# One ring of seven for weight and conditioning tiles, and the shifted S5 inputs regrouped through DRAM, in a two-layer trunk on one core

## The chip, the cores and the metric

The kernel runs on one core of one Trainium2 chip. The metric is device time in microseconds (us). Before the change it is 2463.67 us, the median of three runs (2461.16 to 2466.41). One execution was profiled; it took 2467.97 us, of which its span on the chip is 2466.1 us. A tile in this text is one 512 KB load, 128 partitions of 1024 fp32 numbers, unless it is called something else.

## The reference

Two layers act on x (256 tokens of 2048 numbers). Layer 0 mixes tokens with stick-breaking attention, layer 1 with S5, a diagonal complex state-space layer; each is followed by an MLP with squared ReLU. Every sub-layer is normalised, shifted, scaled and gated by vectors that come from the conditioning vector c.

```python
for i in range(DEPTH):
    mod = cond @ ada_w[i] + ada_b[i]
    sh1, sc1, g1, sh2, sc2, g2 = jnp.split(mod, 6, axis=-1)
    h = modulate(rmsnorm(x, ln1_g[i]), sh1, sc1)
    y = stick_breaking_mixer(...) if i == 0 else s5_mixer(...)
    x = x + g1[:, None, :] * y
    h = modulate(rmsnorm(x, ln2_g[i]), sh2, sc2)
    x = x + g2[:, None, :] * sq_relu_mlp(h, mlp_w1[i], mlp_w2[i])
```

S5 projects h to u (`w_in`), groups 16 channels to a state of 64 complex numbers, runs the recurrence over the tokens, adds `d_skip * u`, applies GELU and then a gated linear unit (`w_glu`), whose result is y. All weights are fp32, so one execution reads some 600 MB.

## The kernel before

Two streams of tiles come in from HBM on one queue, that of SyncE (SP).

**Weights.** `weights` (L126) loads a tile into `w`, ScalarE (ACT) copies it to `wh`, a rounded fp32r number, and VectorE (DVE) takes the difference `wl` (L133). TensorE (PE) then multiplies three times: `wl` by the high part, `wh` by the low part and `wh` by the high part of the activations. One call of `cols_tile` (L152) is one tile and 24 such matmuls, and ends a tick of the program (`tick`, L101). `w` has three buffers (`self.nw = 3`), `wh` and `wl` have three each (`self.nh`).

**Conditioning.** `ada_load` (L262) loads tiles of `ada_w` into `adaw`, a ring of its own with four buffers (eight in the first stage). DVE multiplies each by one number per partition and adds it to a running sum (L356, L370): one instruction and one tile are a unit. `pump` (L240) hands out units at `self.rate` per tick: 1.0 from the first MLP on, 0.42 after the function `between`, 0.35 in the S5 mixer, and in the GLU `pace(44, ...)`, which spreads what is still missing over 44 ticks. `drain` does at once what has to be ready.

The order within PE and POOL is as written. On SP, ACT and DVE a scheduler places each instruction by its readiness and by when a buffer of its ring comes free, and the queue then runs in that order, each instruction waiting for those ahead of it.

The stages are attention (to about 496 us), the first MLP (256 tiles, here MLP0), S5 (32 tiles of `w_in`), GLU (64 tiles of `w_glu`) and the second MLP (256 tiles, MLP1).

**S5.** Eight groups of four ticks each give `acc`, in which two blocks of 128 channels stand; there are 16 blocks `bi`. For each block a plan of delays, counted in ticks (`at`), issues:

- `s5_windows`: DVE scales `acc` into `u` (L1029), ACT adds the shift (L1030). Four zero columns stand ahead of the 256 tokens.
- `s5_shuffle`, one tick later: 16 matmuls against columns of the identity move four channel groups and four shifts of u into PSUM, and ACT copies them to `imc` (L1040). [...]
- `s5_operands`, one tick later as well, and `s5_states`, two ticks later: eight matmuls of `imc` (L1053) and then seven DVE instructions (L1055 to L1063, with the scan L1060). The table T that they read is loaded on SP (L1000) into a ring of two.
- `s5_outputs`, six ticks later, and `s5_taps`, four ticks later.

```python
for q in range(4):
    for j in range(4):
        nc.tensor.matmul(pi[32 * j:32 * j + 32, 65 * q:65 * q + 65], self.ident[:, 32 * q:32 * q + 32],
                         uw[:, 4 - j:4 - j + 257:4], start=True, stop=True)
```

Of the kernel before, what the change touches and what calls it, by code (L numbers as in the profile page):

```python
# [8 lines left out]
F32 = mybir.dt.float32  # L9
# [3 lines left out]
AF = mybir.ActivationFunctionType  # L13
OP = mybir.AluOpType
AX = mybir.AxisListType

P = 128
D = 2048
NB = D // P
S = 256  # L20
# [36 lines left out]
class Trunk:  # L57
# [203 lines left out]

    def ada_load(self, layer, vec, g, t, wide=False):  # L262
        start = g == 0 and vec < 2 and layer == 0
        wt = (self.ap0 if start else self.wp).tile([P, 2, 512], F32, name="adaw", bufs=8 if start else 4)
        c0 = vec * D + g * 512
        w = self.i["ada_w"][layer]
        if wide:
            self.nc.sync.dma_start(wt, w[t * P:t * P + P, c0:c0 + 1024].rearrange("p (a b) -> p a b", a=2))
        else:
            self.nc.sync.dma_start(wt, w[2 * t * P:2 * t * P + 2 * P, c0:c0 + 512].rearrange("(a p) b -> p a b", p=P))  # L270
        return wt
# [630 lines left out]
    def s5_open(self, sp):  # L902
        g_ = self.nc.gpsimd
        self.sE = sp.tile([P, 2, 4, 4, 2, 16], F32, name="E")
        self.sCA = [sp.tile([P, 2, 4, 4, 2, 16], F32, name="CA%d" % k) for k in range(3)]
        self.sKL = [sp.tile([P, 3, 4, 2, 16], F32, name="KL%d" % k) for k in range(3)]
        self.simc = [sp.tile([P, 4, 65], F32, name="imc%d" % k) for k in range(3)]
        self.sU = [sp.tile([P, 4 + S + 1], F32, name="u%d" % k) for k in range(3)]
        self.sM = [sp.tile([P, 2, 4, 64], F32, name="M%d" % k) for k in range(2)]
        self.sP = [sp.tile([P, 224], F32, name="taps%d" % k) for k in range(2)]  # L910
        for t in [self.sE] + self.sP + self.sM + self.sCA + [u[:, 0:4] for u in self.sU]:
            g_.memset(t, 0.0)
        self.sS = {}

# [108 lines left out]
            nc.tensor.transpose(pk[:, tau * P - P:tau * P], self.sP[bi % 2][:, o:o + P], self.ident)  # L1023
        nc.scalar.activation(self.sKL[bi % 3].rearrange("p t q a e -> p (t q a e)"), pk[:, :3 * P], AF.Copy)

    def s5_windows(self, bi, acc):
        nc = self.nc
        uw = self.sU[bi % 3]
        nc.vector.tensor_tensor(uw[:, 4:], acc[:, :S + 1], self.rms, op=OP.mult)  # L1029
        nc.scalar.activation(uw[:, 4:4 + S], uw[:, 4:4 + S], AF.Identity, bias=uw[:, 4 + S:])  # L1030

    def s5_shuffle(self, bi):
        nc = self.nc
        uw, imc = self.sU[bi % 3], self.simc[bi % 3]
        pi = self.mp()
        for q in range(4):
            for j in range(4):
                nc.tensor.matmul(pi[32 * j:32 * j + 32, 65 * q:65 * q + 65], self.ident[:, 32 * q:32 * q + 32],  # L1038
                                 uw[:, 4 - j:4 - j + 257:4], start=True, stop=True)
        nc.scalar.activation(imc.rearrange("p q k -> p (q k)"), pi[:, :4 * 65], AF.Copy)  # L1040

    def s5_states(self, sp, bi):
        nc, s5 = self.nc, self.s5
# [20 lines left out]

    def s5_outputs(self, sp, bi):
        nc = self.nc
        u, St = self.sU[bi % 3][:, 4:4 + S], self.sS.pop((bi, "R")).rearrange("p c (q k) -> p c q k", q=4)
        CA, KL, imc = self.sCA[bi % 3], self.sKL[bi % 3], self.simc[bi % 3]
        py = self.mp()
        for tau in range(4):  # L1070
            for c in range(2 if tau == 0 else 3):
                for q in range(4):
                    o = py[32 * q:32 * q + 32, 64 * tau:64 * tau + 64]
                    if c < 2:
                        lhs, rhs = CA[:, c, q, tau], St[:, c, q]
                    else:
                        lhs, rhs = KL[:, tau - 1, q], imc[:, q, 1:65]
                    nc.tensor.matmul(o, lhs.rearrange("p a e -> p (a e)"), rhs, start=(c == 0), stop=(c == (2 if tau else 1)))  # L1078
        nc.vector.scalar_tensor_tensor(u.rearrange("p (k i) -> p i k", i=4), u.rearrange("p (k i) -> p i k", i=4),
                                       self.dcol[:, bi:bi + 1], py[:, 0:S].rearrange("p (i k) -> p i k", i=4),  # L1080
                                       op0=OP.mult, op1=OP.add)
        nc.scalar.activation(self.z[:, bi], u, AF.Gelu_apprx_tanh)
        if not self.split_z:
            self.sdone.add(bi)
        else:
            self.split(self.hH[:, bi, :S], self.hL[:, bi, :S], self.z[:, bi])

    def s5_mixer(self, mid):
        nc, tc = self.nc, self.tc
        w_in, w_glu = self.i["s5_w_in"][0], self.i["s5_w_glu"][0]  # L1090
        st = ExitStack()
        sp = st.enter_context(tc.tile_pool(name="s5", bufs=1, reuse_waits="tile"))
# [7 lines left out]
        for gi in range(8):  # L1100
            acc = self.accs()
            if gi < 7:
                self.at(2, self.s5_load, sp, gi + 1)
            for b in range(2):
                bi = 2 * gi + b
                t = 4 + 2 * b
                self.at(t + 6, self.s5_outputs, sp, bi)
                self.at(t - 0, self.s5_expand, sp, bi)
                self.at(t, self.s5_windows, bi, acc[:, b])
                self.at(t + 1, self.s5_operands, sp, bi)  # L1110
                self.at(t + 1, self.s5_shuffle, bi)
                self.at(t + 2, self.s5_states, sp, bi)
                self.at(t + 4, self.s5_taps, bi)
            for t in range(4):
                self.cols_tile(acc, w_in, gi * 256, t, hH, hL)
# [16 lines left out]
        a, b = self.gemm_two(w_glu, D, 0, *z, before)  # L1132
        with tc.tile_pool(name="glu", bufs=2, reuse_waits="tile") as gp:
            for g in range(8):
# [4 lines left out]
                if g:  # L1139
                    b = self.gemm_cols(w_glu, g * 256, *z)  # L1140
# [41 lines left out]

    def run(self):
        nc = self.nc
        self.nw, self.nh = 3, 3
        self.rate, self.credit, self.pending = 0.0, 0.0, {}
        self.recorder, self.early = None, True
        self.left, self.acts, self.unit, self.sums, self.turn = {}, [], 0, None, 0
# [56 lines left out]

        self.mlp(0, nxt=ready, between=between)
        self.dump("x2")
        self.rate = 0.35
        self.s5_mixer(mid)
        self.dump("x3")  # L1250
        self.logexp()
# [32 lines left out]
```

## Time and profile before

| what | value |
|---|---|
| median of three runs | 2463.67 us |
| profiled execution, and its span | 2467.97 us, 2466.1 us |
| PE busy | 2365.1 us (96%) |
| DVE busy | 1795.4 us (73%) |
| ACT busy | 1212.7 us (49%) |
| POOL busy | 316.6 us (13%) |
| read from HBM | 607 MB, with the rest 253 GB/s over the span |

PE is shown busy for 96% of the span. These ends are modelled and matmuls overlap, so the number of matmul records in a stretch says more than the busy time; some records can be missing. DMA is the busy share of the 16 DMA engines. `PEclk` is the granted TensorE clock as a part of 2.4 GHz. A row such as "PE acc L160 <- DVE wl L133" says that PE stood idle and what released it. Idle time of an engine off the path costs nothing, and a busy share is an average over stages that differ.

### The profile page before, as it was taken

The numbers are of one execution on the slowest core, as the hardware profiler recorded it, in microseconds if no ns is written. First come the engines' busy times: TensorE is split into PE (matmuls) and PEld (weight loads), VectorE is DVE, ScalarE is ACT, GpSimd is POOL, SyncE is SP. The second block draws the span as 40 slices with busy tenths as digits, with TensorE's granted clock in tenths as the row PEclk, the third lists the DMA queues.
The fourth block names the chain that finished last, engine by engine and source line by source line (L and its number), as shares of the span: only waits on it lengthen the run. The fifth ranks groups of instructions, "written<-read, shape, count | busy, mean of one in ns | idle before, by whom it ended". The sixth has DMA issues, their size and how long they took to land.

```text
span 2466.1 us, 45235 instructions
## 1 busy us (share of the span) xinstructions
PE 2365.1 (96%) x18355; PEld 2160.4 (88%) x18355; DVE 1795.4 (73%) x2223; ACT 1212.7 (49%) x1814; POOL 316.6 (13%) x340
## 2 busy tenths in 40 slices
PE   7999999999998999889999999989999999999999
PEld 4777789899988899889998998989998998998987
DVE  5789999999778767875786668888744554555554
ACT  4534875346334335435546776434554543543543
POOL 0000110001056545445300000000000000000000
PEclk9999999999999999999999999999999999999999
DMA  9888899999999967997798544999856555556565
GB/s 341 302 299 306 288 308 320 322 303 294 310 310 315 300 207 230 309 299 219 259 316 276 174 154 159 314 329 314 281 175 192 184 186 190 175 179 193 180 195 164
DMA packets 416773, 627.09 MB, mean 254 GB/s; under 512 B 19858, under 2 KB 282420, under 8 KB 414260
## 3 DMA queue, kind: packets, MB, share of 16 engines
q1 hardware_dynamic: 411968, 606.16, 74.8%
q0 software_dynamic: 3968, 17.83, 2.2%
q8 instruction: 144, 2.36, 0.4%
q14 instruction: 65, 0.53, 0.1%
q10 hardware_dynamic: 628, 0.21, 0.0%
HBM read 607.34 MB, written 16.78 MB: 253 GB/s over the span
## 4 chain that ended last, share of the span: by engine, by line
PE 44%; DMA 6%; DVE 5%; issue 3%; ACT 0%; SPq 0%; DVEq 0%; ACTq 0%
PE acc L160 9%; PE acc L162 8%; PE acc L161 8%; DMA adaw<-in_ada_w 5%; PE acc L146 5%; PE acc L148 5%; PE acc L147 5%; DVE wl L133 2%; PE mp L1053 1%; DVE adsums L356 1%; PE mp L1078 1%; PE mp L1038 1%; PE mp L1015 1%; DVE xT L435 1%; DMA w<-in_s_w_glu 0%
## 5 line engine op out<-in xcount | busy, mean ns | idle before, releaser
L131 ACT ACTIVATE wh<-w 128x1024 fp32r<-128x1024 f32 x736 | 777.5, 1058 | 1030.9 <-PE acc L162 364.6
L133 DVE TENSOR_TENSOR wl<-w,wh 128x1024 fp32r<-128x1024 f32 x736 | 922.6, 1255 | 436.9 <-ACT wh L131 434.3
L160 PE MATMUL acc<-hH,wl 128*128 128x258 f32 (+1 forms) x2816 | 808.4, 287 | 28.4 <-DVE wl L133 26.1
L162 PE MATMUL acc<-hH,wh 128*128 128x258 f32 (+1 forms) x2816 | 799.2, 284 | 0.0
L161 PE MATMUL acc<-hL,wh 128*128 128x258 f32 (+1 forms) x2816 | 797.8, 283 | 0.2 <-DVE hL L123 0.2
L160 PEld LDWEIGHTS acc<-hH,wl 128*128 128x128 f32 x2816 | 535.8, 190 | 44.3 <-DVE wl L133 33.6
L161 PEld LDWEIGHTS acc<-hL,wh 128*128 128x128 f32 x2816 | 536.3, 190 | 0.6 <-DVE hL L123 0.4
L162 PEld LDWEIGHTS acc<-hH,wh 128*128 128x128 f32 x2816 | 534.8, 190 | 0.0
L160 PE MATMUL acc<-aH,wl 128*128 128x256 f32 x1024 | 294.3, 287 | 26.4 <-DVE wl L133 25.5
L161 PE MATMUL acc<-aL,wh 128*128 128x256 f32 x1024 | 289.5, 283 | 0.0
L162 PE MATMUL acc<-aH,wh 128*128 128x256 f32 x1024 | 289.4, 283 | 0.0
L356 DVE SCALAR_TENSOR_TENSOR adsums<-adaw,cond,adsums 128x1024 f32<-128x1024 f32 x150 | 199.1, 1328 | 53.6 <-DMA adaw<-in_ada_w 53.0
L160 PEld LDWEIGHTS acc<-aH,wl 128*128 128x128 f32 x1024 | 194.3, 190 | 34.1 <-DVE wl L133 33.7
L146 PE MATMUL acc<-wh,aL 128*128 128x512 f32 x512 | 202.2, 395 | 0.0
L148 PE MATMUL acc<-wh,aH 128*128 128x512 f32 x512 | 202.1, 395 | 0.0
L147 PE MATMUL acc<-wl,aH 128*128 128x512 f32 x512 | 202.0, 395 | 0.0
L161 PEld LDWEIGHTS acc<-aL,wh 128*128 128x128 f32 x1024 | 194.4, 190 | 0.0
L162 PEld LDWEIGHTS acc<-aH,wh 128*128 128x128 f32 x1024 | 194.2, 190 | 0.0
L370 DVE SCALAR_TENSOR_TENSOR adacc<-adaw,cond,adacc 128x512 f32<-128x512 f32 x240 | 179.2, 750 | 3.1 <-DMA adaw<-in_ada_w 1.3
L146 PE MATMUL acc<-wh,hL 128*128 128x512 f32 x384 | 157.5, 410 | 5.8 <-ACT wh L131 3.1
L147 PE MATMUL acc<-wl,hH 128*128 128x512 f32 x384 | 153.8, 401 | 3.3 <-DVE wl L133 3.2
L148 PE MATMUL acc<-wh,hH 128*128 128x512 f32 x384 | 152.9, 398 | 0.0
(311 smaller groups left out, 2751.0 us busy)
## 6 DMA issues: line engine op xcount, KB each, us to landing
w<-in_mlp_w SPq DMA_DIRECT2D x512, 512.0 KB, 4.0
adaw<-in_ada_w SPq DMA_DIRECT2D x384, 512.0 KB, 6.0
w<-in_sb_w_in SPq DMA_DIRECT2D x96, 512.0 KB, 5.2
w<-in_s_w_glu SPq DMA_DIRECT2D x64, 512.0 KB, 5.4
w<-in_sb_w_out SPq DMA_DIRECT2D x32, 512.0 KB, 5.7
w<-in_s_w_in SPq DMA_DIRECT2D x32, 512.0 KB, 4.8
pw<-W POOLq DMA_DIRECT2D x8, 1024.0 KB, 6.5
W<-pw SPq DMA_DIRECT2D x8, 1024.0 KB, 7.7
```

Of the source, the lines that this page charges most:

```text
L131: nc.scalar.activation(h, w, AF.Copy)
L133: nc.vector.tensor_tensor(l, w, h.bitcast(F32), op=OP.subtract)
L146: nc.tensor.matmul(o, aL(kb)[:, s], H[:, kk], start=(kb == k0), stop=False)
L147: nc.tensor.matmul(o, aH(kb)[:, s], L[:, kk], start=False, stop=False)
L148: nc.tensor.matmul(o, aH(kb)[:, s], H[:, kk], start=False, stop=(kb == k1 - 1))
L160: nc.tensor.matmul(o, L[:, kk, s], aH(kb), start=(kb == k0), stop=False)
L161: nc.tensor.matmul(o, H[:, kk, s], aL(kb), start=False, stop=False)
L162: nc.tensor.matmul(o, H[:, kk, s], aH(kb), start=False, stop=(kb == k1 - 1))
L356: nc.vector.scalar_tensor_tensor(acc, wt, c, acc, op0=OP.mult, op1=OP.add)
L370: nc.vector.scalar_tensor_tensor(acc, wt[:, kk], c, acc, op0=OP.mult, op1=OP.add)
L435: nc.vector.scalar_tensor_tensor(x, y, self.mod[layer][:, vec * 16 + kb:vec * 16 + kb + 1], x, op0=OP.mult, op1=OP.add)
L1015: nc.tensor.transpose(pe[:, q * P:q * P + P], E[:, c, q].rearrange("p j a e -> p (j a e)"), self.ident)
```

## The change

Three things change.

1. `adaw` outside the first stage is no ring of its own any more: conditioning tiles and weight tiles take turns in one ring `w` of seven buffers (`self.nw = 7`). It holds as many bytes as the three and four before.
2. The shuffle on PE goes. `s5_inputs` scales into a scratch tile `uw` (one buffer), ACT writes u with the four token phases apart (`i k`) and stores it in DRAM (`um`) from its own queue. `s5_regroup`, one tick later, reads it back on SP in four pieces, one for each shift. Column 0 of `imc` stays zero. `s5_states` comes three ticks after the inputs, where it came after two.
3. The rate of conditioning units in the S5 mixer is 0.6, where it was 0.35.

`s5_outputs` now reads u and PSUM in the same order and leaves the reordering to the GELU on ACT.

```diff
 def ada_load(self, layer, vec, g, t, wide=False):
     start = g == 0 and vec < 2 and layer == 0
-    wt = (self.ap0 if start else self.wp).tile([P, 2, 512], F32, name="adaw", bufs=8 if start else 4)
+    wt = self.ap0.tile([P, 2, 512], F32, name="adaw", bufs=8) if start else self.wp.tile([P, 2, 512], F32, name="w", bufs=self.nw)
...
-        self.sU = [sp.tile([P, 4 + S + 1], F32, name="u%d" % k) for k in range(3)]
+        self.sU = [sp.tile([P, S], F32, name="u%d" % k) for k in range(3)]
+        self.um = [self.dram.tile([P, S], F32, name="um%d" % bi) for bi in range(16)]
...
-        for t in [self.sE] + self.sP + self.sM + self.sCA + [u[:, 0:4] for u in self.sU]:
+        for t in [self.sE] + self.sP + self.sM + self.sCA + self.simc:
             g_.memset(t, 0.0)
...
-    def s5_windows(self, bi, acc):
-        nc = self.nc
-        uw = self.sU[bi % 3]
-        nc.vector.tensor_tensor(uw[:, 4:], acc[:, :S + 1], self.rms, op=OP.mult)
-        nc.scalar.activation(uw[:, 4:4 + S], uw[:, 4:4 + S], AF.Identity, bias=uw[:, 4 + S:])
-
-    def s5_shuffle(self, bi):
-        nc = self.nc
-        uw, imc = self.sU[bi % 3], self.simc[bi % 3]
-        pi = self.mp()
-        for q in range(4):
-            for j in range(4):
-                nc.tensor.matmul(pi[32 * j:32 * j + 32, 65 * q:65 * q + 65], self.ident[:, 32 * q:32 * q + 32],
-                                 uw[:, 4 - j:4 - j + 257:4], start=True, stop=True)
-        nc.scalar.activation(imc.rearrange("p q k -> p (q k)"), pi[:, :4 * 65], AF.Copy)
+    def s5_inputs(self, sp, bi, acc):
+        nc = self.nc
+        uw, u = sp.tile([P, S + 1], F32, name="uw", bufs=1), self.sU[bi % 3]
+        nc.vector.tensor_tensor(uw, acc[:, :S + 1], self.rms, op=OP.mult)
+        nc.scalar.activation(u.rearrange("p (i k) -> p i k", i=4), uw[:, :S].rearrange("p (k i) -> p i k", i=4), AF.Identity, bias=uw[:, S:])
+        nc.scalar.dma_start(self.um[bi], u)
+
+    def s5_regroup(self, bi):
+        nc, imc = self.nc, self.simc[bi % 3]
+        src = self.um[bi].rearrange("(q p) (i k) -> i p q k", q=4, i=4)
+        for j in range(4):
+            o = 1 if j else 0
+            nc.sync.dma_start(imc[32 * j:32 * j + 32, :, o:o + 64], src[(4 - j) % 4])
...
-        nc.vector.scalar_tensor_tensor(u.rearrange("p (k i) -> p i k", i=4), u.rearrange("p (k i) -> p i k", i=4),
-                                       self.dcol[:, bi:bi + 1], py[:, 0:S].rearrange("p (i k) -> p i k", i=4),
-                                       op0=OP.mult, op1=OP.add)
-        nc.scalar.activation(self.z[:, bi], u, AF.Gelu_apprx_tanh)
+        nc.vector.scalar_tensor_tensor(u, u, self.dcol[:, bi:bi + 1], py[:, 0:S], op0=OP.mult, op1=OP.add)
+        nc.scalar.activation(self.z[:, bi].rearrange("p (k i) -> p i k", i=4), u.rearrange("p (i k) -> p i k", i=4), AF.Gelu_apprx_tanh)
...
-                self.at(t, self.s5_windows, bi, acc[:, b])
+                self.at(t, self.s5_inputs, sp, bi, acc[:, b])
                 self.at(t + 1, self.s5_operands, sp, bi)
-                self.at(t + 1, self.s5_shuffle, bi)
-                self.at(t + 2, self.s5_states, sp, bi)
+                self.at(t + 1, self.s5_regroup, bi)
+                self.at(t + 3, self.s5_states, sp, bi)
...
-        self.nw, self.nh = 3, 3
+        self.nw, self.nh = 7, 3
...
-        self.rate = 0.35
+        self.rate = 0.6
         self.s5_mixer(mid)
```

The order of the loads on SP shows what the one ring does. The first place is MLP0, from its 64th weight tile on; `in_ada_w` is a conditioning tile, `in_mlp_w` a weight tile. Before:

```order
L268 DMA adaw<-in_ada_w 128x1024
L129 DMA w<-in_mlp_w 128x4x256
L268 DMA adaw<-in_ada_w 128x1024
L129 DMA w<-in_mlp_w 128x4x256
L268 DMA adaw<-in_ada_w 128x1024
L129 DMA w<-in_mlp_w 128x4x256 x2
L268 DMA adaw<-in_ada_w 128x1024
L129 DMA w<-in_mlp_w 128x4x256
```

The same place now:

```order
L268 DMA w<-in_ada_w 128x1024
L129 DMA w<-in_mlp_w 128x4x256 x3
L268 DMA w<-in_ada_w 128x1024
L129 DMA w<-in_mlp_w 128x4x256 x2
L268 DMA w<-in_ada_w 128x1024
L129 DMA w<-in_mlp_w 128x4x256 x2
L268 DMA w<-in_ada_w 128x1024
L129 DMA w<-in_mlp_w 128x4x256 x3
```

Before, conditioning tiles had run ahead of the rate of 0.42 and stood nearly one to one with weight tiles, with long runs of weight tiles alone elsewhere. Now they stand at the rate. Counted over the whole listing, MLP0 has 146 conditioning tiles before and 117 now, S5 has 7 and 20, GLU has 59 and 60, MLP1 has 17 and 32.

The second place is the middle of S5 on SP; `in_s_w_in` is a weight tile, T and W are tables of S5. Before, from the 17th weight tile on:

```order
L917 DMA W<-pw_5451 128x2048
L1000 DMA T<-rot_5436 128x768
L129 DMA w<-in_s_w_in 128x4x256 x2
L1000 DMA T<-rot_5437 128x768
L129 DMA w<-in_s_w_in 128x4x256 x2
L917 DMA W<-pw_5452 128x2048
```

Now, where the number behind `um` counts the blocks:

```order
L1039 DMA imc_14058<-um_14067 32x4x64 x4
L1001 DMA T<-rot_5437 128x768
L268 DMA w<-in_ada_w 128x1024
L129 DMA w<-in_s_w_in 128x4x256
L918 DMA W<-pw_5452 128x2048
L1039 DMA imc_14059<-um_14068 32x4x64 x4
L129 DMA w<-in_s_w_in 128x4x256
L1001 DMA T<-rot_5438 128x768
L268 DMA w<-in_ada_w 128x1024
L129 DMA w<-in_s_w_in 128x4x256
```

Four reads of `imc` and one or two conditioning tiles have come into each block. When the reads of a block are issued, three to seven weight tiles beyond its own group of four ticks have been issued ahead of them.

The third place is the end of GLU (`in_s_w_glu`) and the start of MLP1 on SP. Before:

```order
L129 DMA w<-in_s_w_glu 128x4x256
L268 DMA adaw<-in_ada_w 128x1024
L129 DMA w<-in_s_w_glu 128x4x256
L268 DMA adaw<-in_ada_w 128x1024
L129 DMA w<-in_mlp_w 128x4x256 x2
L268 DMA adaw<-in_ada_w 128x1024
L129 DMA w<-in_mlp_w 128x4x256
```

Now:

```order
L268 DMA w<-in_ada_w 128x1024 x2
L129 DMA w<-in_s_w_glu 128x4x256
L268 DMA w<-in_ada_w 128x1024
L129 DMA w<-in_s_w_glu 128x4x256
L268 DMA w<-in_ada_w 128x1024
L129 DMA w<-in_s_w_glu 128x4x256 x21
L129 DMA w<-in_mlp_w 128x4x256 x5
```

The 60 conditioning tiles of GLU now stand among its first 43 weight tiles, and the last 21 stand alone. Before, the first 8 weight tiles stood alone and the 59 were spread over the rest.

## Rows read from the trace of the kernel before

**Rows 1.** Windows: us; busy (x) of PE, PEld, DVE, ACT, POOL; clock, DMA, GB/s.
```profile
20.00:320.00 300.00, 288.40 (x1322) 216.61 (x1321) 254.50 (x438) 166.72 (x325) 11.04 (x17) 0.98 0.89 305
...
620.00:1290.00 670.00, 633.17 (x5166) 621.48 (x5165) 513.61 (x510) 291.24 (x359) 273.09 (x274) 0.99 0.85 279
1290.00:1530.00 240.00, 232.71 (x3602) 215.77 (x3605) 168.92 (x233) 162.54 (x329) 5.13 (x11) 0.99 0.58 186
1530.00:1800.00 270.00, 252.32 (x2123) 246.85 (x2112) 221.48 (x245) 121.79 (x160) 0.00 (x0) 0.98 0.90 306
1800.00:2466.00 666.00, 660.07 (x4058) 590.52 (x4056) 346.59 (x319) 302.73 (x348) 0.00 (x0) 1.00 0.59 183
```

**Rows 2.** Waits of PE in 620:1290: us in total, times, longest.
```profile
PE acc L160 <- DVE wl L133: 35.9, 30, 3.2
```

**Rows 3.** Windows: two stretches of 60 us within MLP0.
```profile
1020.00:1080.00 60.00, 52.31 (x422) 50.28 (x421) 48.73 (x45) 17.62 (x18) 38.35 (x36) 1.00 0.92 306
...
1140.00:1200.00 60.00, 60.00 (x504) 60.00 (x503) 37.72 (x38) 33.06 (x44) 21.71 (x23) 1.00 0.68 210
```

**Rows 4.** Waits in 1020:1080.
```profile
ACT wh L131 <- DMA w<-in_mlp_w: 33.2, 14, 5.4
```

**Rows 5.** Windows of 620:1290 for L356, then for L133: us, DVE busy (x).
```profile
620.00:1290.00 670.00, 144.03 (x103) 0.99 0.85 279
...
620.00:1290.00 670.00, 280.46 (x212) 0.99 0.85 279
```

**Rows 6.** Timeline of PE in S5: start us, us, then the instruction.
```profile
1401.32 1.13 PE L1038 MATMUL mp<-u,ident 128*32 128x65 f32 x32
1402.38 0.39 PE L160 MATMUL acc<-hH,wl 128*128 128x258 f32 x1
...
1413.55 1.13 PE L1038 MATMUL mp<-u,ident 128*32 128x65 f32 x32
```

**Rows 7.** Groups of instructions on DVE: busy us, mean ns of one.
```profile
L133 DVE TENSOR_TENSOR wl<-w,wh 128x1024 fp32r<-128x1024 f32 x736 | 922.6, 1255 | 436.9 <-ACT wh L131 434.3 <-PE acc L162 0.7
...
L356 DVE SCALAR_TENSOR_TENSOR adsums<-adaw,cond,adsums 128x1024 f32<-128x1024 f32 x150 | 199.1, 1328 | 53.6 <-DMA adaw<-in_ada_w 53.0
...
L1060 DVE TENSOR_TENSOR_SCAN R<-M,R 128x512 f32<-128x512 f32 x16 | 19.6, 1224 | 0.7
...
L1055 DVE TENSOR_TENSOR w<-mp,T 128x512 f32<-128x512 f32 x16 | 11.0, 690 | 12.7 <-PE mp L1053 12.7
...
L1079 DVE SCALAR_TENSOR_TENSOR u<-u,colv,mp 128x256 f32<-128x256 f32 x16 | 10.9, 682 | 0.0
```

**Rows 8.** Groups of the split on ACT and of the S5 inputs.
```profile
L131 ACT ACTIVATE wh<-w 128x1024 fp32r<-128x1024 f32 x736 | 777.5, 1058 | 1030.9 <-PE acc L162 364.6 <-DMA w<-in_mlp_w 240.3 <-PE acc L148 236.7
...
L1030 ACT ACTIVATE u<-u 128x256 f32<-128x256 f32 x16 | 8.1, 508 | 15.2 <-DVE u L1029 15.2
...
L1029 DVE TENSOR_TENSOR u<-acc,rms 128x257 f32<-128x257 f32 x16 | 6.7, 420 | 9.9 <-PE acc L162 9.3 <-ACT z L1082 0.5
```

**Rows 9.** DMA issues: count, KB each, median us from issue to landing.
```profile
rot<-turns POOLq DMA_DIRECT2D x16, 384.0 KB, 4.9
T<-rot SPq DMA_DIRECT2D x16, 384.0 KB, 3.6
```

**Rows 10.** Timeline of the SP queue: start us, us that one issue takes.
```profile
1500.56 0.34 SPq L1000 DMA_DIRECT2D T<-rot  x1
```

**Rows 11.** Waits of the SP queue over the whole span.
```profile
SPq L1000 <- DVE w L1062: 60.2, 13, 5.6
```

**Rows 12.** Windows within GLU.
```profile
1540.00:1720.00 180.00, 167.96 (x1364) 163.19 (x1364) 152.52 (x173) 73.47 (x94) 0.00 (x0) 0.99 0.93 318
1590.00:1650.00 60.00, 51.17 (x411) 49.54 (x411) 56.81 (x72) 23.86 (x34) 0.00 (x0) 0.99 1.01 357
```

**Rows 13.** Windows of 1590:1650 for L133, then for L356.
```profile
1590.00:1650.00 60.00, 19.51 (x16) 0.99 1.01 357
...
1590.00:1650.00 60.00, 29.03 (x24) 0.99 1.01 357
```

More of the change, by code (lines that the diff above doesn't have):

```diff
@@ L1066, in s5_outputs @@
         nc = self.nc
-        u, St = self.sU[bi % 3][:, 4:4 + S], self.sS.pop((bi, "R")).rearrange("p c (q k) -> p c q k", q=4)
+        u, St = self.sU[bi % 3], self.sS.pop((bi, "R")).rearrange("p c (q k) -> p c q k", q=4)
         CA, KL, imc = self.sCA[bi % 3], self.sKL[bi % 3], self.simc[bi % 3]
```

## The prediction

> **What bounds the kernel now.** I read the windows by stage first, then PE's waits within a stage, then the loads behind them. The reader should see four regimes in [rows 1]. Attention (20:320) has DVE busy 254.5 of 300 us. MLP0 and GLU (620:1290, 1530:1800) have the DMA engines busy 85% and 90%, with PE below full. S5 (1290:1530) and MLP1 (from 1800 on) have them at 58% and 59%, and MLP1 has PE at 660.07 of 666 us: there is nothing to gain there.
>
> In MLP0 PE's only wait is for `wl`, 35.9 us in 30 pieces [rows 2]. Two stretches of it tell why. From 1140 to 1200, where no conditioning tile is read, PE makes 504 matmul records in 60 us, 0.119 us each, so a tile of 24 costs 2.86 us [rows 3]. From 1020 to 1080 it makes 422, at 306 GB/s and 92% DMA share [rows 3], and ACT waits 33.2 us for weights that have not landed [rows 4]. The loss is 82 records, 9.8 us of 60. So conditioning tiles in bursts starve PE while other stretches have room.
>
> **MLP0: the one ring.** The stage made 5166 records in 670 us [rows 1]; at 0.119 us they need 615 us, so 55 us are lost. It consumed 212 weight and 103 conditioning tiles [rows 5], 0.49 to one on average, but nearly one to one where the order before bunches them. Now they stand at 0.43, evenly (seven to sixteen in the listing). Demand, worked out: 212 + 92 tiles of 0.524 MB in 615 us are 259 GB/s. To this comes other traffic: 279 GB/s times 670 us are 187 MB, less 315 tiles (165 MB) leaves 22 MB, 36 GB/s. Together 295 GB/s, below the 357 GB/s that the DMA engines reach in GLU [rows 12], though not far below the 306 of the starved stretch [rows 3]. DVE then needs 1.26 us per weight tile and 0.43 x 1.33 us for conditioning [rows 7], 1.83 of 2.86 us. What hid nothing before was the depth: with three weight buffers a late tile showed at once; now about five of the seven hold weights.
>
> Of the 55 us I take back 30 of the 35.9 us of waits, 4 of the 6.7 us that a granted clock of 0.99 over 670 us means (parts of it ran at the lower level, 1.2 GHz), and 2 of the 12 us left, which the trace does not explain: 36 us. The bounds are 15 (the DMA engines still late half of the time, since 295 is near 306) and 52 (all but the small rest).
>
> **S5: PE's part.** The shuffle of a block starts at 1401.32 and the next tile at 1402.38, so it holds PE for 1.06 us [rows 6]; 16 of them are 17 us. The eviction to `imc` on ACT goes too, on an engine that is not late. The blocks follow each other every 12.23 us (1401.32 to 1413.55) [rows 6]; without the shuffle, 11.17.
>
> What stands beside it: DVE has per block two `wl` (2.51 us), the scan (1.22), six multiplies and adds like L1055 (0.69 each, 4.14), the scaling (0.42, [rows 8]), the output (at most 0.68) and, new, 20 conditioning tiles over 16 blocks (1.25 x 1.33 = 1.66) [rows 7]. That is 10.63 of 11.17 us, 95%, on a queue that waits in order for PE's states. I expect 0.4 us lost per block, 7 us, so S5 gives 10 us. Bounds: 17 given, or a loss if the round trip is late (below).
>
> **S5: the round trip.** The wait that is new sits on SP: the four reads wait for the store, and weights queue behind them. The trace before has no such store from ACT; the nearest rows are the store of 384 KB from POOL, 4.9 us, and the read of T on SP, 3.6 us [rows 9]. The chain is 0.42 (DVE) + 0.51 (ACT) + one `wh` ahead of the store (1.06) [rows 8] + 4.9 + 3.6 = 10.5 us, and 4 x 0.34 = 1.4 us for issuing four reads [rows 10]: 11.9 us. Against it, PE has three tiles (8.6 us) and at least one full set of S5 work (11.17 - 5.72 = 5.45 us) between inputs and states: 14 us. So it fits by 2 us for the first block of a group; the second has two ticks more. For the weights behind the reads the cover is larger: three to seven tiles beyond the group are issued ahead of them. That SP can stand still is shown: it waits 60.2 us in 13 pieces for T's buffer [rows 11], while PE in S5 is 232.71 of 240 us busy. I take nothing for this wait; its upper bound is rival B.
>
> On this the Trainium skill speaks against the change: "DMA: Bandwidth & Descriptors", section "Anatomy of one DMA", says that a transfer's signal comes only when the last byte is confirmed, which takes longest where HBM is the target. No row here shows a small store to HBM alone. By that section's fit (2.0 us plus bytes over 436 GB/s; an estimate) the store would take 2.3 and the reads 2.1 us, the chain 7.8 us, and rival B would be less likely; its caution about HBM pulls the other way.
>
> **GLU: what comes back.** Conditioning work not done early in MLP0 falls here. From 1540 to 1720 PE made 1364 records where 180 us allow 1513, so 17.7 us are lost now [rows 12]. From 1590 to 1650, 24 conditioning and 16 weight tiles go through DVE [rows 13] in 60 us at 101% DMA share: 1.5 us per tile of either kind, DVE at 56.81 of 60 [rows 12]. That is the price of this mixture on both engines. Now 60 conditioning tiles stand among 43 weight tiles: 103 x 1.5 = 155 us against 43 x 2.86 = 123, 32 lost instead of 17.7, less some 2 us for what the ring holds when the stage begins: 12 us worse. Bounds: 0 (the seven buffers smooth it) and 25 (DVE's order adds to it).
>
> **The rest.** At the end of GLU DVE is free of conditioning, so the sum of squares that PE waits for should come sooner: 2 us. MLP1 gets 15 conditioning tiles more over half its ticks, under a DMA share of 59%: nothing. Attention keeps its 139 tiles and its DVE time: nothing, plus or minus 6.
>
> **Sum.** -36 - 10 + 12 - 2 = -36 us on the profiled 2467.97, so 2432 there. The profiled run lies 4.3 us above the median, which gives 2463.67 - 36 = 2428 us.
>
> **Rivals.**
> - A, the DMA engines bound MLP0 whatever the order. For it: 306 GB/s was all that the starved stretch got, with POOL's tables moving beside. Against it: GLU ran at 357. MLP0 gives 15 instead of 36: 2449 us.
> - B, slower: the round trip sets the pace of S5. Place: the states on PE, which wait for `imc`, with DVE and its `wl` in order behind. For it: the margin is 2 us, and SP already waits up to 5.6 us for T [rows 11]; 11.9 + 5.6 = 17.5 us are 3.5 too late, 16 times, 56 us. That gives -36 + 56 = +20: 2484 us. It decides from 36 / 16 = 2.3 us of lateness per block. Against it: the second block of each group has more room, and T's wait precedes only some reads.
> - C, DVE becomes the bound in S5 and GLU, at 95% in both: S5 gives 0, GLU costs 25. -36 + 0 + 25 - 2 = -13: 2451 us.
> - D, everything fits: -52 - 17 + 5 - 4 = -68: 2396 us.
> That the ring does nothing is no rival, since the order on SP has changed as shown.
>
> **How the numbers follow.** Forecast 0.58, A 0.14, C 0.12, B 0.08, D 0.08. The forecast's own range is 2410 to 2446. The 8-in-10 range runs from 2398 to 2458: it takes in A and C and half of D and leaves out B. No change means within 0.2%, 4.9 us, about what a measurement can tell. Faster: the forecast, D, and nine tenths of A and C less a little, 0.86. Within 0.2%: the upper edges of A and C and a quarter of B, 0.06. Slower: most of B and the rest, 0.08.
>
> **What would show it.** Right: in MLP0 PE's wait for `wl` falls from 35.9 us to under 10 with 0.43 conditioning tiles per weight tile; blocks in S5 follow each other at 11.2 to 11.8 us; in GLU PE loses some 30 us in its first two thirds and none in its last; MLP1 is unchanged. Wrong: PE waiting for `imc`, or SP waiting for the store while ACT waits for weights (B); 306 GB/s and the old waits in MLP0 (A); a block of 12 us in S5 with DVE never idle (C). If MLP0 gives less than 20 us or S5 takes longer than before, the forecast fails at that step.

## The result: 2.7% slower

| | before | after |
|---|---|---|
| median, us (runs) | 2463.99 (4) | 2530.32 (4), 2526.79 to 2537.05 |
| ratio, 95% interval | | 1.0273 [1.0248, 1.0298] |
| span of the profiled run, us | 2466.1 | 2525.0 |

The forecast was 2428 us, with a range of 2398 to 2458. The stages below are differences between first starts in the timelines: the evictions to `half` (first group of MLP0), the first `rl` of its second group, the first S5 input (L1029, after: L1030), the first and the last `sg` of GLU.

| us | attention | MLP0, first group | MLP0, rest | S5 | GLU | rest |
|---|---|---|---|---|---|---|
| before | 503.1 | 214.3 | 607.5 | 211.2 | 186.9 | 743.1 |
| after | 498.5 | 217.1 | 662.9 | 217.9 | 187.3 | 741.3 |

The medians are 66.3 us apart, the two profiled executions 58.9. Of these 58.9 us, 55.4 lie in MLP0 behind its first group, where 36 were to be won, and 6.7 in S5, where 10 were.

### The profile page after: what moved, and what is told of

Read it like the earlier page. It is cut to its first block, busy times and chain, and to the rows that moved or that the text cites. A ratio compares the mean times of both kernels' runs of the same rounds, so it can differ in the third digit from the quotient of the medians.

```text
span 2525.0 us, 44340 instructions
## 1 busy us (share of the span) xinstructions
PE 2364.2 (94%) x17843; PEld 2160.1 (86%) x17843; DVE 1781.1 (71%) x2223; ACT 1211.9 (48%) x1798; POOL 306.0 (12%) x340
## 4 chain that ended last, share of the span: by engine, by line
PE 34%; DMA 6%; issue 5%; DVE 4%; ACT 2%; SPq 1%; POOLq 0%; POOL 0%; DVEq 0%; ACTq 0%
PE acc L160 6%; PE acc L162 6%; PE acc L161 6%; PE acc L147 5%; PE acc L148 5%; PE acc L146 5%; DMA w<-in_s_w_in 2%; DMA w<-in_ada_w 2%; DVE wl L133 1%; DMA um<-u 1%; DMA w<-in_s_w_glu 1%; ACT wh L131 1%; DVE adsums L356 0%; ACT CA L995 0%; DMA W<-pw 0%
## 5 line engine op out<-in xcount | busy, mean ns | idle before, releaser
L133 DVE TENSOR_TENSOR wl<-w,wh 128x1024 fp32r<-128x1024 f32 x736 | 917.9, 1255 | 308.6 <-ACT wh L131 307.4
L356 DVE SCALAR_TENSOR_TENSOR adsums<-w,cond,adsums 128x1024 f32<-128x1024 f32 x150 | 196.2, 1308 | 193.3 <-DMA w<-in_ada_w 192.8
L370 DVE SCALAR_TENSOR_TENSOR adacc<-w,cond,adacc 128x512 f32<-128x512 f32 x240 | 179.8, 752 | 3.5 <-DMA w<-in_ada_w 1.3
```

What stands on the lines that cost most here:

```text
L133: nc.vector.tensor_tensor(l, w, h.bitcast(F32), op=OP.subtract)
L356: nc.vector.scalar_tensor_tensor(acc, wt, c, acc, op0=OP.mult, op1=OP.add)
L370: nc.vector.scalar_tensor_tensor(acc, wt[:, kk], c, acc, op0=OP.mult, op1=OP.add)
```

## The profile after

Windows of MLP0 and of two stretches of it, answering to [rows 1, 3], then S5 before and after, last most of GLU after (us; busy and count of PE, PEld, DVE, ACT, POOL; clock, DMA share, GB/s). S5 and GLU lie later by then, so their windows are those of the stage and not the same times as before:

```profile
620.00:1290.00 670.00, 590.47 (x4671) 576.06 (x4670) 430.88 (x428) 262.52 (x318) 260.03 (x274) 0.97 0.74 238
1020.00:1080.00 60.00, 53.83 (x432) 52.98 (x431) 40.57 (x40) 23.93 (x29) 21.19 (x21) 0.97 0.72 231
1140.00:1200.00 60.00, 52.41 (x404) 51.33 (x402) 37.27 (x36) 23.58 (x29) 28.68 (x29) 0.94 0.76 240
...
1325.00:1536.00 211.00, 206.97 (x3461) 190.18 (x3462) 151.91 (x208) 145.25 (x294) 0.00 (x0) 1.00 0.54 170
...
1378.00:1596.00 218.00, 193.52 (x2937) 181.18 (x2936) 170.94 (x228) 145.42 (x281) 0.00 (x0) 0.96 0.69 224
...
1600.00:1780.00 180.00, 165.83 (x1333) 160.85 (x1333) 141.03 (x164) 72.47 (x93) 0.00 (x0) 0.98 0.89 303
```

MLP0 makes 495 matmul records less in the same 670 us, some 59 us at 0.119 us each [rows 3]. DVE is busy 83 us less, and the DMA engines 74% instead of 85%: no engine is the bound. PE's waits for `wl` in this window are 78.0 us (below) instead of 35.9 [rows 2], and a granted clock of 0.97 instead of 0.99 over 670 us is some 13 us more: an estimate that leaves little over. The stretch that ran best before (504 records, now 404) is as bad as the other (422, now 432): the loss is spread evenly.

Waits from 720 to 1340 of the SP queue, then of DVE, last of PE in 620:1290, which answers to [rows 2] (us in total, times, longest):

```profile
SPq L129 <- DMA w<-in_ada_w: 168.7, 61, 6.4
SPq L129 <- DVE wl L133: 150.0, 106, 5.8
SPq L268 <- DVE wl L133: 75.3, 67, 3.4
...
DVE adsums L356 <- DMA w<-in_ada_w: 109.3, 39, 6.9
DVE adacc L356 <- DMA w<-in_ada_w: 70.2, 25, 5.3
...
PE acc L160 <- DVE wl L133: 78.0, 49, 5.3
```

The same rows of SP and DVE before:

```profile
SPq L129 <- DVE wl L133: 401.8, 181, 5.8
...
DVE adsums L356 <- DMA adaw<-in_ada_w: 21.9, 19, 3.6
DVE adacc L356 <- DMA adaw<-in_ada_w: 9.4, 10, 1.9
```

The first row after is the one to see. L129 issues a weight; it has stood 168.7 us for the landing of a conditioning tile, which it does not need, and 86.3 us more (50.4 in 37 pieces and 35.9 in 26) until DVE had read that tile. In the kernel before no wait for a conditioning tile's landing exists on SP: it waits 401.8 us for `wl`, as a ring of three weights should. DVE's waits for the landing of conditioning tiles were 21.9 and 9.4 us; they are 109.3 and 70.2. One case of it, the timeline of SP and DVE (start us, us; in brackets the idle time before; SP's second row spans two issues):

```profile
918.03 0.39 SPq L268 DMA_DIRECT2D w<-in_ada_w  x1
919.60 6.05 SPq L129 DMA_DIRECT2D w<-in_mlp_w  x2
...
923.97 1.28 DVE L356 SCALAR_TENSOR_TENSOR adsums<-w,cond,adsums 128x1024 f32<-128x1024 f32 x1 [4.39 <-DMA w<-in_ada_w]
925.17 0.68 DVE L565 TENSOR_TENSOR half<-half,acc 128x512 f32<-128x512 f32 x1
925.76 1.22 DVE L133 TENSOR_TENSOR wl<-w,wh 128x1024 fp32r<-128x1024 f32 x1
...
927.04 0.39 PE L160 MATMUL acc<-hH,wl 128*128 128x258 f32 x1 [1.67 <-DVE wl L133]
```

A conditioning tile is issued at 918.03, a weight at 919.60; the next weight goes out only at 925.28, as soon as DVE has read that conditioning tile (923.97 to 925.25). It was given this tile's buffer. Meanwhile DVE stood 4.39 us for the landing with a `wl` behind it in order, and PE then 1.67 us for that `wl`. From 925 to 932 the DMA engines moved 211 GB/s, from 918 to 925 342.

The buffers in the built program confirm it. A pool with one name and seven buffers is not used in turn: by their addresses a load often gets the one that was filled last but one, or last but two. The likely reason, which no run tests, is that the scheduler hands out what its own plan frees first, and a conditioning tile is read by DVE alone. In MLP0 92 of 373 loads stand in the buffer of a conditioning tile issued two or three loads before (81 of them weights), and 275 of the others in one filled seven to ten loads before; in the kernel before, no load stands so near behind a conditioning tile.

A short distance need not cost anything. In MLP1 all 32 conditioning tiles of the changed kernel hand their buffer on to a weight at most three loads later. SP waits for their landing there too, but 25.7 us in 27 pieces (1790 to 2466), PE waits for nothing, and what follows GLU takes 741.3 us instead of 743.1. Four or five weights stand between two such tiles there, 11.4 to 14.3 us of PE's work at 2.86 us each [rows 3]. In MLP0 it is two or three, 5.7 to 8.6 us, while from the issue of such a tile to the issue of the load in its buffer 6.5 us pass in the median of the 92. That the loss begins where this time no longer fits under PE's work is an estimate, which no run tests.

## The experiments

All times in us. "MLP0" is its part after the first group. "Short" counts loads of the whole MLP0 in the buffer of a conditioning tile issued at most three loads before; "cond." counts the conditioning tiles among S5's loads.

| run | median | ratio to before [95%] | attention | MLP0 | short | S5 | cond. | GLU |
|---|---|---|---|---|---|---|---|---|
| e1_two_rings | 2447.97 | 0.9931 [0.9905, 0.9956] | 501.0 | 606.0 | 0 | 195.2 | 7 | 177.3 |
| e2_ring_only | 2529.53 | 1.0263 [1.0247, 1.0279] | 499.7 | 660.6 | 92 | 217.2 | 12 | 188.3 |
| e3_fixed_turns | 2479.86 | 1.0060 [1.0045, 1.0075] | 529.2 | 597.3 | 23 | 222.8 | 20 | 190.9 |
| e4_regroup_only | 2449.70 | 0.9935 [0.9918, 0.9952] | 503.3 | 607.3 | 0 | 199.4 | 7 | 182.6 |
| e5_reads_on_pool | 2461.87 | 0.9981 [0.9961, 1.0001] | 498.8 | 606.4 | 0 | 215.2 | 7 | 178.8 |
| e8_ring_reads_on_pool | 2541.49 | 1.0320 [1.0300, 1.0340] | 501.5 | 662.4 | 92 | 234.0 | 20 | 182.5 |
| e9_w4_a3 | 2471.75 | 1.0042 [1.0029, 1.0054] | 512.2 | 606.8 | 0 | 211.4 | 8 | 184.1 |
| e10_w6_a1 | 3013.83 | 1.2232 [1.2194, 1.2269] | 872.5 | 632.2 | 145 | 237.5 | 17 | 292.5 |
| e11_no_cond_in_s5 | 2526.87 | 1.0259 [1.0243, 1.0274] | 499.9 | 661.5 | 92 | 195.6 | 2 | 209.5 |
| e12_more_cond_two_rings | 2455.34 | 0.9975 [0.9959, 0.9991] | 499.7 | 602.9 | 0 | 211.4 | 13 | 177.1 |
| e13_w2_a5 | 2723.03 | 1.1044 [1.1022, 1.1066] | 537.2 | 707.0 | 0 | 197.8 | 0 | 206.9 |
| e14_ring_of_six | 2566.60 | 1.0425 [1.0405, 1.0445] | 510.8 | 681.2 | 94 | 220.1 | 20 | 190.7 |
| e15_fixed_turns_six | 2577.91 | 1.0464 [1.0449, 1.0480] | 552.9 | 649.1 | 73 | 226.1 | 19 | 191.9 |
| e16_s5_free | 2443.68 | 0.9924 [0.9912, 0.9936] | 500.4 | 602.4 | 0 | 194.3 | 0 | 184.5 |

### Which part of the change

**e1_two_rings**, against the changed kernel:

```
-        wt = ... else self.wp.tile([P, 2, 512], F32, name="w", bufs=self.nw)
+        wt = (self.ap0 if start else self.wp).tile([P, 2, 512], F32, name="adaw", bufs=8 if start else 4)
-        self.nw, self.nh = 7, 3
+        self.nw, self.nh = 3, 3
```

> The changed kernel with the two rings of the kernel before (three buffers for weights, four for conditioning tiles); the regrouping by store and reads and the rate 0.6 stay. The order of MLP0's loads is then that of the kernel before (146 conditioning tiles). Theory (the shared ring makes SP wait for a conditioning tile that it issued two or three loads earlier, and this alone costs the time): the 55 us lost in MLP0 are all back, the wait of SP for a conditioning tile before it may issue the next load (168.7 us in 61 pieces from 720 to 1340) is gone there, and the kernel comes to 2450 to 2475 us, about the kernel before. Rival 1 (the regrouping on the weights' queue is the cause, with some of its waits in MLP0's end and attention): stays over 2500 us. Rival 2 (cause shared by ring and regrouping): 2480 to 2500.

**e2_ring_only**, the two lines of the change put into the kernel before (`name="w", bufs=self.nw` for both kinds of tile, `self.nw` 7).

> The kernel before with the shared ring of seven alone: the shifted inputs are still made by matmuls, the rate is still 0.35. MLP0's loads then stand as in the changed kernel (117 conditioning tiles, a weight in the buffer of a conditioning tile issued two or three loads before, 62 times). Theory (the shared ring is the whole of the loss): 2510 to 2535 us, with DVE waiting some 180 us for conditioning tiles between 720 and 1340 as in the changed kernel. Rival 1 (the regrouping is the cause): 2455 to 2470. Rival 2 (both): 2480 to 2500.

**e4_regroup_only**: e1_two_rings with `self.rate = 0.35`.

> The kernel before with the regrouping by store and reads alone: two rings of three and four, rate 0.35. Beside the run with rate 0.6 it tells what the rate does. Theory: S5's 16 blocks lose 17 us of PE work and get back part of it in waits (in the changed kernel PE waits 7.4 us in 4 pieces for the regrouped inputs and SP 100.5 us in 15 pieces for the store): S5 takes 200 to 215 us instead of 211, the kernel 2450 to 2470 us, and within 5 us of the same kernel at rate 0.6. Rival (the queue standing still for the store starves PE with only three weight buffers): S5 takes 225 us or more and the kernel over 2475 us.

The ring alone gives 66 us more than before, the whole loss; the regrouping alone gives 14 to 15 us less, and S5 falls by 12 to 16. The rate is worth nothing that can be told (2447.97 against 2449.70, the runs overlap). All three theories held; e1 and e4 came out a little under their 2450 (e4 also under its 200 us in S5), so the regrouping is a gain where no ring is shared.

### Why the ring costs

**e3_fixed_turns**, against the changed kernel:

```
+    def ring(self, shape):
+        self.place = (self.place + 1) % self.nw
+        return self.wp.tile(shape, F32, name="w%d" % self.place, bufs=1)
-        w = self.wp.tile([P, a, b], F32, name="w", bufs=self.nw)
+        w = self.ring([P, a, b])
```

> The changed kernel, but the seven buffers are taken strictly in turn (seven names with one buffer each), so that a load waits for the tile that was placed seven tiles before and not for one issued two or three loads earlier; 117 conditioning tiles in MLP0 and the regrouping as in the changed kernel. Theory (which buffer a load is given costs the time, not the even order nor the count of seven): MLP0 from its second group on falls from 663 us to 590 to 620 us, SP's wait for conditioning tiles falls under 60 us, and the kernel comes to 2440 to 2490 us. Rival (the even order of conditioning tiles among weights, with DVE taking them in order, costs the time whatever the buffers): 2515 us or more, with DVE's wait for conditioning tiles near its 180 us.

MLP0 falls from 662.9 to 597.3 us with the same count of buffers and the same 117 conditioning tiles: 65.6 us hang on which buffer a load gets, and on what the scheduler makes of it. The order is not the same, though the expectation's two theories take it to be: in the changed kernel one weight alone stands between two conditioning tiles 16 times and more than three never, in e3 one 66 times and four to seven 18 times. So the rival, that the even order costs something by itself, is not excluded by this run; no run has the even order of MLP0 with buffers in real turns. SP's waits for conditioning tiles from 720 to 1340, where L272 loads a conditioning tile and L133 a weight, answer to the 168.7 us above, which a weight now stands 10.3:

```profile
SPq L272 <- DMA w<-in_ada_w: 40.1, 24, 6.8
...
SPq L133 <- DMA w<-in_ada_w: 10.3, 11, 2.1
```

Against the kernel before (607.5) MLP0 is 10 us shorter, with 29 conditioning tiles fewer in it. But attention takes 26 us more than before and MLP0's first group 16.7 less (197.6), so that the second group starts 9.4 us later: of the 10 us little is left. A window of attention, 20 to 200, has PE at 158.29 us with 688 records and a clock of 0.93, where two rings have 173.58, 794 and 0.98, and ACT waits for attention's weights. Why fixed turns do this there was not separated.

**e14_ring_of_six** is the changed kernel with `self.nw` 6, **e15_fixed_turns_six** is e3 with 6. (The counts of short distances in their expectations cover a part of MLP0; the table has all.)

> The changed kernel with a shared ring of six instead of seven; 117 conditioning tiles in MLP0 in the same even order, a weight in the buffer of a conditioning tile issued two or three loads before, 66 times instead of 62. Theory (the short distance, not the number of buffers, makes SP stand still): MLP0 655 to 675 us, the kernel 2525 to 2545 us, within 1% of the ring of seven. Rival (the buffers in all, weights and conditioning, are what the ring lacks): one less costs a like share, MLP0 over 685 us.

> The ring with fixed turns, of six buffers instead of seven. With the free ring one buffer less cost MLP0 18 us (662.9 to 681.2), which neither view had expected. In this one a weight takes the buffer of a conditioning tile issued two loads before 30 times in MLP0 (none with fixed turns of seven, 62 and 66 times with the free rings of seven and six). Theory (the short distance costs about 1 us each time, the buffers in all some 18 us apart from it): MLP0 597 + 30 + 18 = 645 us, between 630 and 655. Rival 1 (only the number of buffers counts once turns are fixed): 605 to 618 us. Rival 2 (the distance alone): 620 to 630.

The ring of six fell between both views: a buffer less costs 18 us at an almost equal count of short distances. With fixed turns of six MLP0 came to 649.1 where the sum of both effects said 645. That fits a cost of both, but the order changed here as well (six weights in a row 22 times), so how the loss divides is not shown. Short distances of conditioning tiles seem to cost less than those of weights: e3 has 23, all conditioning, and e10 below 145, all conditioning, with 632.2 us; the ring of seven has 92, 81 of them weights, with 662.9.

**e9_w4_a3**, **e10_w6_a1**, **e13_w2_a5**: two rings of other sizes (e9 and e10 with the reads on POOL's queue as in e5, e13 with them on SP).

```
-        ... name="adaw", bufs=8 if start else 4)
+        ... name="adaw", bufs=8 if start else 3)
-        self.nw, self.nh = 3, 3
+        self.nw, self.nh = 4, 3
```

> Seven buffers in two rings again, but four for weights and three for conditioning tiles, reads on POOL's queue. The load order stays near that of the kernel before (145 conditioning tiles in MLP0, in the same bunches); a conditioning tile takes the buffer of one issued six or seven loads before. Theory (what counts is that no load waits for a tile issued two or three before it; a fourth weight buffer then covers part of the 29.5 us that PE waits for weights in MLP0): MLP0 590 to 606 us, the kernel 2425 to 2448 us. Rival (three conditioning buffers hold SP back as the shared ring does): MLP0 over 620 us, the kernel over 2460.

> Seven buffers in two rings, six for weights and one for conditioning tiles, reads on POOL's queue. Weights now go round six deep (a weight takes the buffer of one issued nine or ten loads before), conditioning tiles stand evenly, one after each two weights (146 in MLP0), and each takes the buffer of the one issued two or three loads before: the short distance of the shared ring, put on conditioning tiles alone. Theory (SP stands still for a conditioning tile that it has just issued, and the weights behind it on the queue are late whatever buffers they have): SP waits over 150 us for conditioning tiles in MLP0, MLP0 takes 640 to 680 us, the kernel 2485 to 2530 us. Rival (the weights' depth is what counts, and six deep rides over such a stop): MLP0 under 610 us, the kernel under 2455.

> Two rings again, two buffers for weights and five for conditioning tiles, regrouping on SP, rate 0.6. With one buffer for conditioning tiles attention took 872.5 us instead of 501, with three 512; four weight buffers instead of three left MLP0 at 606.8 against 606.0 us. So conditioning buffers have been worth more than weight buffers. Theory (this goes on): attention 490 to 500 us, MLP0 within 8 us of 606, the kernel 2430 to 2450 us. Rival (two weight buffers leave a load no time to land while the other is used: a tile is used up in some 2.9 us): MLP0 over 640 us, MLP1 longer too, the kernel over 2500 us.

None of the three came out as my theory had it. A fourth weight buffer, taken from the conditioning tiles, left MLP0 at 606.8 us (606.4 with three) and PE's waits for `wl` there at 29.8 us (31.2; 700 to 1340), and three conditioning buffers cost attention 13. With one conditioning buffer and six for weights MLP0 took 632.2 us, below the 640 of the theory and above the 610 of the rival; the big loss lies where conditioning tiles follow each other, 371 us in attention alone and 115 in GLU. SP's waits of that kernel from 20 to 870:

```profile
SPq L270 <- DMA adaw<-in_ada_w: 250.5, 100, 4.4
...
SPq L270 <- DVE adacc L370: 170.9, 110, 5.8
```

Each tile there waits for the one before it to land and be read. Whatever a fifth conditioning buffer gives, two for weights outweigh it: MLP0 is 100 us longer (PE's wait for `wl` is 85.8 us in 68 pieces from 720 to 1390): the rival was right. Three and four is the best split of seven that was run.

### What the regrouping is worth, and where S5 lost it

**e5_reads_on_pool** is e1, **e8_ring_reads_on_pool** the changed kernel, each with

```
-            nc.sync.dma_start(imc[32 * j:32 * j + 32, :, o:o + 64], src[(4 - j) % 4])
+            nc.gpsimd.dma_start(imc[32 * j:32 * j + 32, :, o:o + 64], src[(4 - j) % 4])
```

> Two rings of three and four, regrouping by store and reads, rate 0.6, but the four reads of a block are issued from POOL's queue (5.8 us busy in S5) instead of SP's, so that SP no longer stands still for the store (84.7 us in 15 pieces with the reads on SP). Theory: with two rings PE waits only 6 us in S5, so at most that can be had: S5 188 to 196 us, the kernel 2440 to 2450 us, the same as with the reads on SP within 0.3%. Rival 1 (SP's standing still costs more than PE's waits show, through GLU's first loads): 2425 to 2438. Rival 2 (POOL issues later or slower, and PE waits longer for the regrouped inputs): over 2455.

> The changed kernel with its shared ring, only the four reads of a block from POOL's queue instead of SP's. In the changed kernel S5 took 217.9 us, with two rings 195.2; ring alone with the matmuls 217.2. Theory (the ring and the store compete for one queue: SP stands still 100.5 us of 218 for the store and then has twenty conditioning tiles and its slot waits left): S5 falls to 196 to 208 us and the kernel to 2508 to 2522 us. Rival (the ring's own slot waits set S5's pace, wherever the reads are issued): S5 stays at 213 us or more, the kernel at 2525 us or more. MLP0 stays at 660 us in both.

SP's standing still was not what S5 lost by. It waited 84.7 us in 15 pieces for the store in e1 and 100.5 in 15 in the changed kernel; without that S5 is 16 to 20 us longer in both, as rival 2 of e5 and the rival of e8 had it. The instructions of the reads, and their time from issue to landing, first of e1, then of e5; then S5's window and PE's waits in it, e1 and e5:

```profile
L1039 SPq DMA_DIRECT2D imc<-um x64: 303/424/1500, 1325.5 to 1496.8; - x64
DMA to landing us min/median/max: 1.6/1.8/5.1
...
1321.00:1517.00 196.00, 189.62 (x2957) 178.89 (x2956) 153.93 (x212) 146.98 (x280) 0.00 (x0) 0.99 0.67 217
PE mp L1052 <- DMA imc<-um: 2.4, 4, 1.0
```

```profile
L1039 POOL DMA_DIRECT2D imc<-um x64: 549/549/573, 1322.7 to 1513.2; - x64
DMA to landing us min/median/max: 1.9/3.5/8.3
...
1319.00:1534.00 215.00, 197.60 (x2949) 186.35 (x2950) 153.41 (x212) 147.62 (x278) 34.79 (x64) 0.94 0.62 197
PE mp L1052 <- DMA imc<-um: 12.2, 5, 4.4
```

From POOL a read takes 0.55 us to issue instead of 0.42 and lands 1.7 us later. PE waits for `imc` 12.2 us instead of 2.4, the granted clock of the stage falls from 0.99 to 0.94 (part of it at the lower level, 1.2 GHz), and the same matmuls keep PE busy 8 us longer.

It is not the queue that makes a read land later, but what runs beside it. The trace has the landing of 48 of e1's 64 reads and of all of e5's. Reads during which packets of 1 KB or more (weights, tiles, tables, the next store) moved less than 64 KB landed after 1.8 us in the median from SP (37 of them) and 1.9 from POOL (4); the others after 3.5 us from either (11 and 60). The Trainium skill, "Trainium Kernel Development and Optimization", section "Key Constraints", says that issuing from another queue saves issue time alone, since all run on the same 16 engines; the trace agrees in the landing, alike from both queues beside like traffic, though POOL took longer to issue. The likely reading is that SP's standing for the store, which holds its loads back, had kept the engines free for the reads behind it; no run holds the loads back with the reads on POOL's queue.

**e11_no_cond_in_s5** (changed kernel, rate 0), **e12_more_cond_two_rings** (e1, rate 1.3), **e16_s5_free** (e1, rate 0, and 0.47 instead of 0.42 for MLP0), all in the one line before `self.s5_mixer(mid)`, e16 in that of `between()` as well:

```
-        self.rate = 0.6
+        self.rate = 0.0
```

> The changed kernel with the rate 0 in place of 0.6 in S5: two conditioning tiles stand among S5's loads instead of 20, and 78 instead of 60 in GLU; ring, regrouping and MLP0 stay. It asks why S5 takes 217.9 us with the ring and 195.2 with two rings. Theory (the 20 conditioning tiles do it: they and their slot waits must go through SP in what its standing for the store leaves): S5 190 to 203 us. Rival (the ring itself, through the weights' buffers, or the granted clock after MLP0): S5 212 us or more. GLU is expected 10 to 25 us longer than 187.3 in both; MLP0 stays at 660.

> Two rings of three and four with the regrouping, rate 1.3 instead of 0.6: 13 conditioning tiles among S5's loads instead of 7. The other side of the same question. Theory (conditioning tiles in S5 cost about 1.2 us each there, as 22.7 us for 13 more in the ring would have it, even without a shared ring): S5 200 to 206 us instead of 195.2. Rival (only together with the shared ring's slots do they cost): S5 193 to 198 us. The whole 2440 to 2458 us.

> Two rings of three and four with the regrouping on SP; rate 0.47 instead of 0.42 in MLP0 and 0 instead of 0.6 in S5: 153 conditioning tiles in MLP0 instead of 146, none in S5 instead of 7, the later stages as they are. Theory (in S5 a conditioning tile costs some 2.7 us beside the regrouping, as 195.2 to 211.4 us for six more had it, and in MLP0 little): S5 185 to 193 us, MLP0 604 to 616, the kernel 2430 to 2448 us, the best of all. Rival (MLP0 has no more room for them: each costs 2 us or more there): MLP0 618 us or more and the kernel 2445 to 2460.

With 0, 2 and 7 conditioning tiles and the reads on SP, S5 takes 194.3, 195.6 and 195.2 us (199.4 in e4, also 7), ring or not; with 13 it takes 211.4 in two rings, with 20 in the ring 217.9. So it is conditioning tiles in S5 that eat the regrouping's gain, and not the ring: the theory of e11 held, and in e12 they cost more than it had said (211.4 where 200 to 206 were expected). In e11 the 18 tiles came back in GLU, 22.2 us longer, and the whole stayed at 2526.87. e16 missed its 185 to 193 in S5 by a little (seven tiles cost next to nothing there) and is still the fastest kernel run: 2443.68 us, 0.9924 [0.9912, 0.9936].

## Why the prediction was wrong

**MLP0, -36: the step that failed.** It stands in "What hid nothing before was the depth: with three weight buffers a late tile showed at once; now about five of the seven hold weights". Both halves are wrong. The ring does not hold five weights in turn; it hands 81 weights of MLP0 the buffer of a conditioning tile that was issued two or three loads before, so SP stands until that tile has landed and been read. PE's wait for `wl`, which was to fall under 10 us, rose from 35.9 to 78.0. Instead of 36 us won the term is 55 lost, and e2 shows 53 of it without the rest of the change. And a fourth weight buffer, taken from the conditioning tiles, moved MLP0 by 0.4 us (e9 against e5), so nothing shows that it was depth that the kernel before lacked. Seven buffers in real turns gave MLP0 10 us (e3), short of the lower bound of 15. The demand of 295 GB/s was never put to the test: 238 were moved, where 306 had been had [rows 3].

**S5, -10.** The term was sized about right for the edit that it names, and wrong for the kernel that it stood in. With two rings S5 falls by 11.8 (e4), 16.0 (e1) and 16.9 us (e16), between the 10 and the 17 us of the shuffles. The 0.4 us per block that I took for the 20 conditioning tiles was too little: S5 lost 22.7 us to them (217.9 against 195.2), 1.4 per block. The waits of PE in S5 after, from 1378 to 1596, are 24.4 us in seven groups, these three first, where e1 has 6.1:

```profile
PE acc L160 <- DVE wl L133: 9.6, 4, 4.8
PE mp L1052 <- DMA imc<-um: 7.4, 4, 3.5
PE mp L1077 <- DVE R L1062: 2.7, 1, 2.7
```

So 18.3 of the 22.7 us are waits, and the rest goes with the clock (0.96 against 0.99; PE busy 193.52 against 189.62 us). I had put DVE at 95% of a block and let it go with a small price; it was busy 78% of the stage (170.94 of 218 us), so it was not DVE's time that ran out.

**S5, the round trip.** This held. The store landed after 4.8 us in the median in the changed kernel and 5.6 in e1 (taken: 4.9), the reads after 1.8 in both (3.6), and PE waited 7.4 and 2.4 us for `imc` in all. A margin of about 2 us fits e5: 1.7 us later landing, and issues slower by 0.13 each, use it up. The Trainium skill, "DMA: Bandwidth & Descriptors", section "Anatomy of one DMA — SWDGE (gpsimd) path", gives its fit for DMAs issued from GpSimd; the prediction used it for ACT's and SP's queues. By it the store would land after 2.3 us and a read after 2.1, both estimates; the trace has that for the quickest store (1.7) and for reads that nothing runs beside (1.8 from SP, 1.9 from POOL), not for the store beside loads.

**GLU, +12.** Measured +0.4, at the bottom of its bounds of 0 and 25; with two rings and about as many tiles as before it even fell to 177.3 to 184.5 us. The shape was as told: against 0.119 us a record PE lost some 21 us in the first 124 us of the stage (866 records from 1596, before 905 from 1536, 16 us) and none in the 64 us behind them (536, before 516). The size was not: 21 lost instead of 32, and why is open. The price per tile was about right where tiles were added: 22.2 us for 18 in e11, 1.2 each against 1.5.

**The rest.** Attention and what follows GLU moved by -4.6 and -1.8 us, within the 6 and near the 2 that were said. The first group of MLP0 belongs to the first term; it moved by +2.8.

**The rivals.** None had the cause. B had the sign, by another mechanism: PE waited 7.4 us for `imc`, not 56. A and C asked what the DMA engines and DVE can do at most, and neither was the bound. The sentence "That the ring does nothing is no rival, since the order on SP has changed as shown" closed the question at the wrong place: the order was read, and which buffer each load waits for was not.

## What to carry to other kernels

A shared pool of buffers is not a ring because it was meant as one: before counting its depth, look for each load at which earlier tile frees its buffer and who reads that tile last. A queue that issues in order stands still for the youngest of them, and the sign of it in a profile is a load's issue that waits for the landing of a tile that it does not need. Then see whether the engine at the end waits too: in MLP0 it did, in MLP1 the same sign cost nothing. And where one stage gains by an edit, ask what the same change has moved into its slack: seven conditioning tiles were free in S5, thirteen cost 16 us.

## What the runs showed of the chip that was not expected

- A read of 32 KB landed by what ran beside it and not by the queue that issued it: 1.8 us from SP (e1, 37 reads) and 1.9 from POOL (e5, 4 reads) beside under 64 KB of larger packets, 3.5 us from either beside more (11 and 60 reads).
- A 128 KB store from ACT's queue landed after 1.8 to 7.6 us, median 5.6, in e1 and after 1.7 to 7.8, median 4.8, in the changed kernel.
- With 11 us of waits more in S5 (17.2 in e5, 6.1 in e1) the granted clock went from 0.99 to 0.94, and PE was busy 197.60 instead of 189.62 us for 2949 and 2957 matmul records.
